# Probabilities turned by a transposing DMA instead of TensorE, with spread stores and earlier last loads

## The chip, the cores and the metric

One core of a Trainium2 chip runs the whole program. The metric is the device time of one execution in microseconds (us); a comparison uses several runs of each kernel on one chip. TensorE does matrix products and transposes (PE in the rows, PEld its weight loads), VectorE is DVE, ScalarE is ACT, GpSimd is POOL, and SyncE (SP) issues nearly all DMA transfers.

## The reference

The reference is a decoder trunk of two layers over 1,024 tokens of width 1,024, in float32. Each layer has a mixer with 16 attention heads and then a mixture of experts; a final RMS norm ends the program. Cut to what the change touches:

```
# 8 heads "fox" (d = 64, decay by a cumulated forget gate), 8 heads "mla" (d = 96, values 64)
s = q_i @ k.T * scale                      # per head and block of 128 queries, causal
s = s + cum[q] - cum[k]                    # fox heads only
p = softmax(where(key <= query, s, -inf))
out_i = p @ v
# mixer: rms_norm of each head, concatenate, @ w_o; h = h + mixer(norm(h)); h = h + moe(norm(h))
# end:   out = rms_norm(h) * final_norm, with h = h + gate_0 * y_0 + gate_1 * y_1 of the last experts
```

## The kernel before

To keep float32 accuracy, an operand is split into a high and a low part and a product is made of three matmuls (`mm3`, L194 to L196). Attention operands are split on the way to DRAM and read back, one head at a time, into a tile `op` (`load_ops`, the DMAs at L93 with the name `op`, some 1.5 MB a head; two buffers, so a head's load waits for the last scores of the head two before it).

A layer's mixer first makes norms and projections (the chunks of `w_in`: v, q, k, each in two halves); `late_pools` then queues the jobs of the mla projections (`qj`, `kj`), and `run(jobs, ...)` puts a few between the matmuls. Their results are stored at L93 as FQ, FK, MQ, MQR, MK.

Attention works in units of up to 1,024 score columns: query block 7 alone, then blocks 6 and 0, 5 and 1, 4 and 2, and block 3 of two heads together. Two heads make a **pair** of 9 units; a layer has 8 pairs, 72 units, four pairs of fox heads and then four of mla heads. One unit goes through these steps:

- `scores` (TensorE, L873 and the causal mask L877) into `S` in PSUM, two buffers;
- `row_max` (VectorE, L885), `expo` (ScalarE, L894: the exponential, into `pr` in SBUF, float32);
- `flip` (8 TensorE transposes L902 into PSUM `pt`; ScalarE L904 takes the high half `ph` in float16, VectorE L905 the low half `pl`);
- `values` (TensorE, L916: three 64-column matmuls for each key block, with `ph` or `pl` as weights).

After the last unit of a head, `fin_a`, `fin_b`, `fin_m` and `fin_c` normalise the output and turn it (L928, L930, L939, L946, L953, L957, L959).

The loop over n (L1001 on) writes `scores(n)`, `row_max(n)`, `flip(n - 1)`, `expo(n)`, `values(n - LAG)` with LAG = 2. The order on TensorE, VectorE, ScalarE and GpSimd is as written. SP's queue is ordered by the library's scheduler and then also runs strictly in order: a DMA that waits holds those behind it.

Each expert weight is loaded, split and multiplied in the mixture of experts, which the change leaves alone. At the end `last_a` (L1653 on) adds two rows `y` of the experts' results per 128 tokens (L225), squares (L1657), and the normed rows are stored (L1665, L1666).

Of the kernel before, what the change touches and what calls it, by code (L numbers as in the profile page):

```python
# [20 lines left out]
P = 128  # L21
# [37 lines left out]
LAG = 2  # L59
PRB = 4  # L60
# [21 lines left out]
def kernel(ctx: ExitStack, tc: tile.TileContext, x, positions, attn_norm, w_in, b_f, q_norm, w_uq,  # L82
# [283 lines left out]
    def mixer(l, opened):  # L366
# [3 lines left out]
        FQ = dram.tile([H, 3 * HD + 4, T], F32R, name=f"FQ{l}")  # L370
        FK = dram.tile([H, 2 * HD + 4, T], F32R, name=f"FK{l}")
# [289 lines left out]
        for dst in (FQ[:, 3 * HD:3 * HD + 2], FK[:, 2 * HD + 2:]):  # L661
            move(dst.rearrange("h r (c t) -> h (r c) t", t=P), one)

        def late_pools():
# [78 lines left out]
            jobs.extend(kj)  # L743
# [6 lines left out]
        for ci, (nm, half) in enumerate(chunks):  # L750
            _, wh, wl = cur
            nxt = prepare(base[chunks[ci + 1][0]] + 256 * chunks[ci + 1][1]) if ci + 1 < len(chunks) else None
            if (nm, half) == ("k", 0):
                late_pools()
# [13 lines left out]
            else:  # L768
                for s in range(4):
# [7 lines left out]
                    def take(nm=nm, j=j, cs=cs, ps=ps):  # L777
                        st = stg.tile([P, 2, 512], F32R, name="st")
                        if nm == "q":
                            split(st[:, 0], st[:, 1], ps, FOX_SCALE)  # L780
                        else:
                            split(st[:, 1], st[:, 0], ps)
                        for e in range(2):
                            h, rs = 2 * j + e, slice(e * HD, (e + 1) * HD)
                            if nm == "q":
                                move(FQ[h, HD:3 * HD].rearrange("(b r) t -> r b t", r=HD)[:, :, cs], st[rs])
                                move(FQ[h, 0:HD, cs], st[rs, 0])
                            else:
                                move(FK[h, 0:2 * HD].rearrange("(b r) t -> r b t", r=HD)[:, :, cs], st[rs])

# [3 lines left out]
                    run(jobs, 4 if nm == "k" else 3)  # L794
# [38 lines left out]
        run(jobs, len(jobs))  # L833
# [54 lines left out]
        def expo(u):  # L888
            u["pr"] = att.tile([P, T], F32, name="pr", bufs=PRB)
            for (h, qb, col), nm in zip(u["segs"], u["nm"]):  # L890
                if h // 2 not in zst:
                    zst[h // 2] = att.tile([P, NT, 2], F32, name="zs", bufs=3)
                s = slice(col, col + (qb + 1) * P)
                act.activation(u["pr"][:, s], u["S"][:, s], AF.Exp, bias=nm, accum_out=zst[h // 2][:, qb, h % 2:h % 2 + 1])  # L894

        def flip(u):
            u["ph"] = att.tile([P, NT, P], F16, name="ph")
            u["pl"] = att.tile([P, NT, P], F16, name="pl")
            for q in range(2):
# [760 lines left out]
    for i in range(NT + 1):  # L1660
        if i < NT:
            last_a(i)
        if i:
            ht, ot, rstd = st[i - 1]
            dve.scalar_tensor_tensor(ot, ht, rstd, gb, op0=OP.mult, op1=OP.mult)  # L1665
            sp.dma_start(out[0, (i - 1) * P:i * P], ot)  # L1666
# [43 lines left out]
```

## Time and profile before

| | us |
|---|---|
| median of 3 runs | 1942.1 (1937.24 to 1949.56) |
| the profiled execution, its own time | 1941.36 |
| its span in the trace | 1939.6 |
| first layer: attention, 72 units | about 245 to 486 |
| second layer: attention, 72 units | about 1189 to 1426 |
| experts, first and second layer | 624 to 940, 1560 to 1880 |
| last stage, after the experts | 1880 to 1939.6 |

The trace has the busy time of each engine in any stretch, the granted clock of TensorE (1.00 is 2.4 GHz, 0.50 is 1.2 GHz), the share of time that the 16 DMA engines were busy, and their rate. A row of a stretch holds its start and end, its length, the busy us (and instructions) of PE, PEld, DVE, ACT and POOL, then the granted clock, the DMA share and GB/s. A pair of fox heads takes 29.0 us (303 to 332), a pair of mla heads 31.3 us (392.3 to 423.6).

### The profile page before, as it was taken

The numbers are of one execution on the slowest core, as the hardware profiler recorded it, in microseconds if no ns is written. First come the engines' busy times: TensorE is split into PE (matmuls) and PEld (weight loads), VectorE is DVE, ScalarE is ACT, GpSimd is POOL, SyncE is SP. The second block draws the span as 40 slices with busy tenths as digits, with TensorE's granted clock in tenths as the row PEclk, the third lists the DMA queues.
The fourth block names the chain that finished last, engine by engine and source line by source line (L and its number), as shares of the span: only waits on it lengthen the run. The fifth ranks groups of instructions, "written<-read, shape, count | busy, mean of one in ns | idle before, by whom it ended". The sixth has DMA issues, their size and how long they took to land.

```text
span 1939.6 us, 33742 instructions
## 1 busy us (share of the span) xinstructions
PE 1742.0 (90%) x12509; PEld 1410.5 (73%) x12509; DVE 1362.6 (70%) x2180; ACT 1184.9 (61%) x2254; POOL 587.2 (30%) x849
## 2 busy tenths in 40 slices
PE   7999899999996999999499997999999979999960
PEld 6987678888785777666399876888878757776640
DVE  6463478888336999888565345888863689998855
ACT  4442378888312898878344334888861268888751
POOL 4001145233313334332331021532241243343315
PEclk9999989999997999999799998999999979999995
DMA  5247833453763999999742776344547479999986
GB/s 162 66 114 213 274 134 111 101 121 88 248 210 135 359 357 353 362 353 357 273 156 53 185 242 219 110 121 107 119 144 251 153 268 365 350 347 358 351 298 221
DMA packets 145380, 427.11 MB, mean 220 GB/s; under 512 B 22166, under 2 KB 37564, under 8 KB 142140
## 3 DMA queue, kind: packets, MB, share of 16 engines
q1 hardware_dynamic: 129788, 387.14, 60.5%
q0 software_dynamic: 14336, 33.58, 5.2%
q10 hardware_dynamic: 1088, 4.19, 0.6%
q8 instruction: 100, 1.64, 0.4%
q14 instruction: 68, 0.56, 0.1%
HBM read 347.24 MB, written 94.37 MB: 228 GB/s over the span
## 4 chain that ended last, share of the span: by engine, by line
PE 60%; DMA 24%; DVE 6%; ACT 6%; issue 2%; POOL 1%; SPq 1%; POOLq 0%; ACTq 0%; DVEq 0%
PE ps L194 9%; PE ps L195 9%; PE ps L196 9%; DMA gu<-in_w_gate_dram 8%; PE S L873 8%; DMA gu<-in_w_up_dram 6%; PE pt L902 6%; DMA dn<-in_w_down_dram 6%; PE y L916 3%; PE gu L195 2%; PE gu L196 2%; PE gu L194 2%; ACT pr L894 2%; PE y L1140 1%; DVE nm L885 1%
## 5 line engine op out<-in xcount | busy, mean ns | idle before, releaser
L1482 DVE TENSOR_TENSOR lo<-gu,hi 128x1024 fp32r<-128x1024 f32 x248 | 298.0, 1221 | 42.1 <-ACT hi L1481 41.3
L1481 ACT ACTIVATE hi<-gu 128x1024 fp32r<-128x1024 f32 x248 | 257.9, 1059 | 29.7 <-DMA gu<-in_w_up_dram 21.1
L873 PE MATMUL S<-op 96*128 96x512 f32 (+3 forms) x960 | 228.8, 372 | 18.2 <-DMA op<-FK 11.6
L885 DVE TENSOR_REDUCE nm<-S 128x1 f32<-128x1024 f32 (+7 forms) x256 | 183.1, 752 | 67.2 <-PE S L877 67.2
L195 PE MATMUL gu<-lo,V 128*96 128x512 f32 x512 | 206.0, 402 | 11.9 <-DVE lo L1482 11.5
L894 ACT ACTIVATE pr<-S,nm 128x1024 f32<-128x1024 f32 (+7 forms) x256 | 189.2, 755 | 36.3 <-DVE nm L885 36.1
L194 PE MATMUL gu<-hi,V 128*96 128x512 f32 x512 | 206.8, 404 | 1.2 <-ACT hi L1481 0.6
L196 PE MATMUL gu<-hi,V 128*96 128x512 f32 x512 | 204.0, 399 | 0.9 <-DVE V L185 0.3
L904 ACT ACTIVATE ph<-pt 128x512 f16<-128x512 f32 x288 | 157.3, 601 | 66.6 <-PE pt L902 65.7
L1531 POOL DMA_INDIRECT y<-V,sidx x64 | 81.9, 1280 | 372.8 <-ACT V L1530 359.2
L905 DVE SCALAR_TENSOR_TENSOR pl<-pt,ph 128x512 f16<-128x512 f32 x288 | 184.7, 682 | 8.9 <-ACT ph L904 7.8
L873 PEld LDWEIGHTS S<-op 96*128 96x128 f32 (+1 forms) x960 | 161.3, 196 | 35.7 <-DMA wor<-in_w_o_dram 6.9
L1482 DVE TENSOR_TENSOR lo<-dn,hi 128x1024 fp32r<-128x1024 f32 x128 | 156.1, 1221 | 18.4 <-ACT hi L1481 14.8
L902 PE MATMUL pt<-ident,pr 128*128 128x128 f32 x1152 | 155.2, 278 | 8.6 <-DVE pl L905 3.5
L1481 ACT ACTIVATE hi<-dn 128x1024 fp32r<-128x1024 f32 x128 | 135.0, 1056 | 21.5 <-DMA dn<-in_w_down_dram 21.3
L902 PEld LDWEIGHTS pt<-ident,pr 128*128 128x128 f32 x1152 | 125.4, 143 | 13.9 <-ACT pr L894 13.0
L195 PEld LDWEIGHTS gu<-lo,V 128*96 128x96 f32 x512 | 83.5, 163 | 58.6 <-DVE lo L1482 29.0
L916 PE MATMUL y<-V,ph 128*128 128x64 f16 x2304 | 121.6, 193 | 2.8 <-ACT ph L904 1.6
L916 PEld LDWEIGHTS <-ph 128*128 128x128 f16 x2304 | 116.9, 98 | 5.3 <-ACT ph L904 1.8
L916 PE MATMUL y<-V,pl 128*128 128x64 f16 x1152 | 117.0, 193 | 1.1 <-DVE pl L905 1.0
L196 PEld LDWEIGHTS gu<-hi,V 128*96 128x96 f32 x512 | 83.4, 163 | 38.3 <-DVE V L185 6.2
L175 POOL TENSOR_SCALAR rs_v<-ss 128x1 f32<-128x1 f32 (+1 forms) x44 | 20.6, 468 | 289.6 <-ACT xn L1096 150.5
(363 smaller groups left out, 4366.0 us busy)
## 6 DMA issues: line engine op xcount, KB each, us to landing
gu<-in_w_gate_dram SPq DMA_DIRECT2D x124, 512.0 KB
gu<-in_w_up_dram SPq DMA_DIRECT2D x124, 512.0 KB
dn<-in_w_down_dram SPq DMA_DIRECT2D x60, 1024.0 KB
raw<-in_w_in_dram SPq DMA_DIRECT2D x48, 256.0 KB
h<-ht SPq DMA_DIRECT2D x17, 512.0 KB
FQ<-st SPq DMA_DIRECT2D x32, 256.0 KB
FK<-st SPq DMA_DIRECT2D x32, 256.0 KB
MQ<-st SPq DMA_DIRECT2D x16, 512.0 KB
```

The source lines that it names most:

```text
L194: pe.matmul(ps, sh(kc), mh(kc), start=first and i == 0, stop=False)
L195: pe.matmul(ps, sh(kc), ml(kc), start=False, stop=False)
L196: pe.matmul(ps, sl(kc), mh(kc), start=False, stop=last and i == n - 1)
L873: pe.matmul(o, a[0:k, qs], b[0:k, c0:c0 + n], start=bank not in started, stop=pi == len(passes) - 1 and not diag, skip_group_check=True)
L885: dve.tensor_reduce(nm, u["S"][:, col:col + (qb + 1) * P], axis=AX.X, op=OP.max, negate=True)
L894: act.activation(u["pr"][:, s], u["S"][:, s], AF.Exp, bias=nm, accum_out=zst[h // 2][:, qb, h % 2:h % 2 + 1])
L902: pe.transpose(pt[:, b], u["pr"][:, (4 * q + b) * P:(4 * q + b + 1) * P], ident)
L904: act.activation(u["ph"][:, ks], pt, AF.Copy, scale=P_SCALE)
L905: dve.scalar_tensor_tensor(u["pl"][:, ks], pt, P_SCALE, u["ph"][:, ks], op0=OP.mult, op1=OP.subtract)
L916: pe.matmul(yst[h][:, qb], a[:, b], v[:, kb, h % H, c], start=first_y[h], stop=(kb == qb and s == 2), skip_group_check=True)
L1481: act.activation(h_, raw, AF.Copy)
L1482: eng.tensor_tensor(l_, raw, h_.bitcast(F32), op=OP.subtract)
```

## The change

- The exponentials `pr` are split in SBUF: ScalarE copies all 1,024 columns to the high half `pq[:, 0]` in float16 right behind the exponential, VectorE makes the low half in one instruction of 1,024 columns. One DMA with transposition, issued by SP, then turns the 128 x 2,048 halves of a unit (512 KB) from SBUF to SBUF into `pT`. The 8 TensorE transposes of a unit and the reads of PSUM `pt` are gone.
- LAG is 3 instead of 2, `pr` has 2 buffers instead of 4, `pq` and `pT` 3 each.
- FQ and FK are stored once per half in 128 partitions, with one DMA for a tile of 512 columns, and their extra rows (decay and ones) go to FQC and FKC. A fox head's operands are read with six DMAs, of 64 or 4 partitions, in place of four of 128 or 68.
- Operand loads are written after the unit that uses a head's buffer last (units 4 and 8 of a pair), for the head two later.
- `late_pools` comes one chunk earlier (at the second half of q); four of the eight `kj` jobs move behind the chunks, between the matmuls of the mla values.
- At the end all 16 loads of `y` are written first (16 buffers), and the norm and store of rows i come two steps after their sum instead of one.

```diff
-LAG = 2
-PRB = 4
+LAG = 3
+PRB = 2
...
+        FQC = dram.tile([H, 4, T], F32R, name=f"FQC{l}")
+        FKC = dram.tile([H, 4, T], F32R, name=f"FKC{l}")
...
-            jobs.extend(kj)
+            jobs.extend(kj[:4])
+            late["kj"] = kj[4:]
...
-            if (nm, half) == ("k", 0):
+            if (nm, half) == ("q", 1):
                 late_pools()
...
+                        move((FQ if nm == "q" else FK)[j * P:(j + 1) * P, :, cs], st)
...
-                move(o[:, 0], FQ[h, 0:2 * HD])
-                move(o[:, 2], FK[h, 0:2 * HD])
-                move(o[0:HD + 4, 1], FQ[h, 2 * HD:])
-                move(o[0:HD + 4, 3], FK[h, HD:])
+                hs = slice(h * HD, (h + 1) * HD)
+                move(o[0:HD, 0:2], FQ[hs])
+                move(o[HD:, 0], FQ[hs, 0])
+                move(o[0:HD, 2:4], FK[hs])
+                move(o[HD:, 2], FK[hs, 1])
+                move(o[HD:HD + 4, 1], FQC[h])
+                move(o[HD:HD + 4, 3], FKC[h])
...
         def expo(u):
...
+            act.activation(u["pq"][:, 0], u["pr"], AF.Copy, scale=P_SCALE)
 
         def flip(u):
-            for q in range(2):
-                pt = tps.tile([P, 4, P], F32, name="pt")
-                for b in range(4):
-                    pe.transpose(pt[:, b], u["pr"][:, (4 * q + b) * P:(4 * q + b + 1) * P], ident)
-                ks = slice(4 * q, 4 * q + 4)
-                act.activation(u["ph"][:, ks], pt, AF.Copy, scale=P_SCALE)
-                dve.scalar_tensor_tensor(u["pl"][:, ks], pt, P_SCALE, u["ph"][:, ks], op0=OP.mult, op1=OP.subtract)
+            dve.scalar_tensor_tensor(u["pq"][:, 1], u["pr"], P_SCALE, u["pq"][:, 0], op0=OP.mult, op1=OP.subtract)
+            u["pT"] = att.tile([P, 2 * NT, P], F16, name="pT")
+            sp.dma_start(u["pT"], u["pq"].rearrange("p s t -> p (s t)"), transpose=True)
...
-                for h, _, _ in U[n]["segs"]:
-                    if h not in opnd:
-                        opnd[h] = load_ops(h)
                 scores(U[n])
                 row_max(U[n])
+                if n % 9 in (4, 8) and n < N - 9:
+                    h = 2 * (n // 9) + 2 + (n % 9 == 8)
+                    opnd[h] = load_ops(h)
...
+    for i in range(NT):
+        for j in range(2):
+            sp.dma_start(ys[i][j], y_d[DEPTH - 1][j * T + i * P:j * T + (i + 1) * P])
...
-    for i in range(NT + 1):
+    for i in range(NT + 2):
         if i < NT:
             last_a(i)
+        if i > 1:
+            last_b(i - 2)
```

Three places in the order of the instructions. First SP's queue in the first layer's attention, between two heads' operand loads (`op` is a head's operand tile, `pq` the two halves of a unit's probabilities, `pT` these turned). Before:

```order
L93 DMA op<-FQ_155 128x1024
L93 DMA op<-FK_156 128x1024
L93 DMA op<-FQ_155 68x1024
L93 DMA op<-FK_156 68x1024
L93 DMA op<-FQ_155 128x1024
```

After the change:

```order
L905 DMA_TRANSPOSE pT<-pq 128x16x128 x4
L93 DMA op<-FQ_155 64x2048
L905 DMA_TRANSPOSE pT<-pq 128x16x128
L93 DMA op<-FQ_155 64x1024
L93 DMA op<-FK_156 64x2048
L93 DMA op<-FK_156 64x1024
L93 DMA op<-FQC_157 4x1024
L93 DMA op<-FKC_158 4x1024
L905 DMA_TRANSPOSE pT<-pq 128x16x128 x3
```

SP's queue held operand loads alone; now 9 transposing DMAs of a pair stand among them, one between the first part of a head's load and its other five, the next behind these.

Second, ScalarE in the first layer's attention at the end of a pair, where `fin_c` turns the outputs (L957). Before:

```order
L894 ACTIVATE pr,zs<-S,nm 128x512 x2
L957 ACTIVATE mix<-y_2510,gains 128x256 x2
L904 ACTIVATE ph<-pt 128x512 x2
L894 ACTIVATE pr,zs<-S,nm 128x1024
L957 ACTIVATE mix<-y_2510,gains 128x256 x2
```

After the change:

```order
L898 ACTIVATE pr,zs<-S,nm 128x1024
L899 ACTIVATE pq<-pr 128x1024
L957 ACTIVATE mix<-y_2484,gains 128x256 x2
L898 ACTIVATE pr,zs<-S,nm 128x896
L898 ACTIVATE pr,zs<-S,nm 128x128
L899 ACTIVATE pq<-pr 128x1024
L957 ACTIVATE mix<-y_2484,gains 128x256 x2
```

The copy of the high half stood ahead of the exponential and waited for TensorE's transposes; now it stands behind the exponential, and ahead of the copies of L957.

Third, SP's queue in the last stage (`y` are the experts' results, `out_dram` the output). Before:

```order
L224 DMA y<-y_139 128x1024 x7
L1666 DMA out_dram<-ot 128x1024
L224 DMA y<-y_139 128x1024
L1666 DMA out_dram<-ot 128x1024
L224 DMA y<-y_139 128x1024 x2
```

After the change:

```order
L1612 COMPARE_AND_BRANCH
L1612 UNCONDITIONAL_BRANCH
L199 DMA gb<-in_final_norm_dram 128x1024
L1651 DMA y<-y_139 128x1024 x16
L1667 DMA out_dram<-ot 128x1024 x8
L1713 UNCONDITIONAL_BRANCH
```

Loads and stores took turns; now no load stands behind a store.

## Rows read from the trace of the kernel before

**Rows 1.** The page: the chain that ended last, by engine.

```profile
PE 60%; DMA 24%; DVE 6%; ACT 6%; issue 2%; POOL 1%; SPq 1%; POOLq 0%; ACTq 0%; DVEq 0%
```

**Rows 2.** Busy time by stretch: first fox pair, a fox pair, an mla pair.

```profile
245.00:274.00 29.00, 27.35 (x295) 23.27 (x296) 21.73 (x38) 19.74 (x46) 9.43 (x12) 0.84 0.34 113
303.00:332.00 29.00, 27.44 (x366) 23.87 (x363) 25.74 (x42) 24.82 (x60) 17.67 (x27) 1.00 0.32 115
392.30:423.60 31.30, 30.56 (x384) 27.06 (x384) 25.52 (x42) 25.95 (x62) 11.28 (x21) 1.00 0.53 116
```

**Rows 3.** Groups in the fox pair, 303 to 332: busy, mean ns | idle before, releaser.

```profile
L905 DVE SCALAR_TENSOR_TENSOR pl<-pt,ph 128x512 f16<-128x512 f32 x19 | 12.2, 684 | 0.5 <-ACT ph L904 0.3
L885 DVE TENSOR_REDUCE nm<-S 128x1 f32<-128x1024 f32 (+7 forms) x16 | 11.4, 752 | 1.5 <-PE S L877 1.5
L904 ACT ACTIVATE ph<-pt 128x512 f16<-128x512 f32 x19 | 10.4, 602 | 2.7 <-PE pt L902 2.6
L902 PE MATMUL pt<-ident,pr 128*128 128x128 f32 x72 | 9.7, 277 | 1.0 <-DVE pl L905 0.6
...
L916 PE MATMUL y<-V,ph 128*128 128x64 f16 x147 | 7.9, 193 | 0.2 <-DVE mix L959 0.2
...
L959 DVE SCALAR_TENSOR_TENSOR mix<-y,gains,mix 128x256 fp32r<-128x256 f32 x4 | 1.8, 480 | 1.4 <-ACT mix L957 1.4
```

**Rows 4.** By stretch: before the first scores of the two layers.

```profile
1174.70:1188.90 14.20, 5.39 (x24) 3.87 (x22) 5.49 (x10) 4.73 (x9) 0.00 (x0) 0.78 0.92 289
230.60:245.30 14.70, 5.28 (x24) 3.84 (x22) 5.49 (x10) 4.73 (x9) 0.00 (x0) 0.84 0.89 283
```

**Rows 5.** By stretch: the last stage.

```profile
1887.00:1891.00 4.00, 0.00 (x0) 0.00 (x0) 1.98 (x2) 0.00 (x0) 0.00 (x0) 0.50 1.03 416
1895.00:1899.00 4.00, 0.00 (x0) 0.00 (x0) 3.26 (x3) 0.32 (x2) 3.58 (x6) 0.50 0.41 155
1899.00:1903.00 4.00, 0.00 (x0) 0.00 (x0) 3.05 (x4) 1.15 (x2) 3.28 (x6) 0.50 0.59 195
```

**Rows 6.** What SP's queue waited for in the last stage: us, times, longest.

```profile
SPq L1666 <- DVE ot L1665: 33.2, 8, 9.5
```

**Rows 7.** The page's groups: 1,024-column copy and difference from SBUF to SBUF.

```profile
L1482 DVE TENSOR_TENSOR lo<-gu,hi 128x1024 fp32r<-128x1024 f32 x248 | 298.0, 1221 | 42.1 <-ACT hi L1481 41.3
L1481 ACT ACTIVATE hi<-gu 128x1024 fp32r<-128x1024 f32 x248 | 257.9, 1059 | 29.7 <-DMA gu<-in_w_up_dram 21.1
```

**Rows 8.** By stretch: operand loads of a fox head (302 to 311), an mla head.

```profile
301.00:302.00 1.00, 0.88 (x8) 0.74 (x8) 1.00 (x2) 0.75 (x4) 1.00 (x1) 1.00 0.00 0
302.00:303.00 1.00, 1.00 (x30) 0.99 (x27) 0.82 (x3) 0.90 (x2) 0.75 (x4) 1.00 0.90 156
304.00:305.00 1.00, 1.00 (x12) 0.96 (x12) 0.74 (x2) 0.74 (x3) 0.93 (x2) 1.00 1.02 414
306.00:311.00 5.00, 5.00 (x62) 4.54 (x61) 4.17 (x8) 4.20 (x10) 1.31 (x3) 1.00 0.25 100
347.00:353.00 6.00, 5.87 (x62) 5.09 (x63) 4.58 (x8) 4.94 (x13) 0.48 (x2) 1.00 0.99 213
```

**Rows 9.** Timeline, start and us: the program's first load (512 KB) and its reader.

```profile
0.72 0.40 SPq L403 DMA_DIRECT2D cq<-in_x_dram  x1
...
4.25 1.06 ACT L412 ACTIVATE xn<-cq 128x1024 f32<-128x1024 f32 x1 [2.25 <-DMA cq<-in_x_dram]
```

**Rows 10.** The chain of waits: start, us, one matmul of the mla values.

```profile
230.15 0.23 PE ps L195
```

**Rows 11.** Timeline of the last stage: first loads, last sums, last norm.

```profile
1883.38 3.83 SPq L224 DMA_DIRECT2D y<-y  x7
...
1921.58 2.61 DVE L225 SCALAR_TENSOR_TENSOR gu<-y,gates,gu 128x1024 f32<-128x1024 f32 x2 [0.22 <-DMA y<-y]
...
1928.20 1.28 DVE L1665 SCALAR_TENSOR_TENSOR ot<-gu,rs_d,gb 128x1024 f32<-128x1024 f32 x1 [1.82 <-POOL rs_d L171]
```

More of the change, by code (lines that the diff above doesn't have):

```diff
@@ L570, in forget_d @@
             cs = slice(c * 512, c * 512 + 512)
-            for dst, sgn in ((FQ[:, 3 * HD + 2:, cs], None), (FK[:, 2 * HD:2 * HD + 2, cs], -1.0)):
+            for dst, sgn in ((FQC[:, 2:, cs], None), (FKC[:, 0:2, cs], -1.0)):
                 st = stg.tile([P, 2, 512], F32R, name="st")[0:H]
@@ L660, in mixer @@
         one = trix[0:H, None, P:].to_broadcast([H, 16, P])
-        for dst in (FQ[:, 3 * HD:3 * HD + 2], FK[:, 2 * HD + 2:]):
+        for dst in (FQC[:, 0:2], FKC[:, 2:]):
             move(dst.rearrange("h r (c t) -> h (r c) t", t=P), one)
@@ L793, in mixer @@
                     take()
-                    run(jobs, 4 if nm == "k" else 3)
+                    run(jobs, 3)
             cur = nxt
@@ L823, in mixer @@
         take()
+        run(jobs, len(jobs))
         uk = late["uk"]
@@ L832, in mixer @@
             v_take(vraw2[:, i], ps, NT + i)
-        run(jobs, len(jobs))
+            if i < len(late["kj"]):
+                late["kj"][i]()
         opnd[1] = load_ops(1)
@@ L914, in values @@
                     b = col // P + kb
-                    for s, (a, c) in enumerate(((u["ph"], 0), (u["ph"], 1), (u["pl"], 0))):
-                        pe.matmul(yst[h][:, qb], a[:, b], v[:, kb, h % H, c], start=first_y[h],
+                    for s, (a, c) in enumerate(((0, 0), (0, 1), (NT, 0))):
+                        pe.matmul(yst[h][:, qb], u["pT"][:, a + b], v[:, kb, h % H, c], start=first_y[h],
                                   stop=(kb == qb and s == 2), skip_group_check=True)
@@ L1021, in mixer @@
                 rt, rt_close = open_pool(f"rt{l}", space=PSUM)
-            if EXF and n < N:
-                expo(U[n])
             if 0 <= n - FL < N:
                 flip(U[n - FL])
-            if not EXF and n < N:
+            if n < N:
                 expo(U[n])
@@ L1649 @@
     gb = cb.tile([P, D], F32, name="gb")
+    ys = [[cb.tile([P, D], F32, name="y", bufs=2 * NT) for _ in range(2)] for _ in range(NT)]
+    for i in range(NT):
+        for j in range(2):
+            sp.dma_start(ys[i][j], y_d[DEPTH - 1][j * T + i * P:j * T + (i + 1) * P])
     bcast_row(gb, final_norm)
@@ L1653, in last_a @@
     def last_a(i):
-        ht = combined(DEPTH, i, got[0][i], lambda j: cb.tile([P, D], F32, name="y", bufs=8))
+        ht = got[0][i]
+        for j in range(2):
+            dve.scalar_tensor_tensor(ht, ys[i][j], gates[:, j, i:i + 1], ht, op0=OP.mult, op1=OP.add)
         ot = cb.tile([P, D], F32, name="ot", bufs=4)
@@ L1658, in last_a, with last_b @@
         st[i] = ht, ot, mean_rsqrt(ss, 1.0 / D, 1, "1")
-    for i in range(NT + 1):
+    def last_b(i):
+        ht, ot, rstd = st[i]
+        dve.scalar_tensor_tensor(ot, ht, rstd, gb, op0=OP.mult, op1=OP.mult)
+        sp.dma_start(out[0, i * P:(i + 1) * P], ot)
+    for i in range(NT + 2):
         if i < NT:
             last_a(i)
[L1663 to L1666, printed above, removed]
+        if i > 1:
+            last_b(i - 2)
     cb_close()
```

14 lines of the change are left out of this document (3 added, 11 removed).

## The prediction

> **What bounds the kernel now.** I read the page's top first [rows 1]: TensorE holds 60% of the chain that ended last, DMA 24%, VectorE and ScalarE 6% each. An average says little here, so I read three stages apart: attention, the stretch ahead of it, and the end.
>
> Attention, by stretches of one pair of heads [rows 2]: a pair of fox heads takes 29.0 us with TensorE busy 27.4, VectorE 25.7 and ScalarE 24.8; a pair of mla heads 31.3 us with TensorE busy 30.6. The mla pairs are bound by TensorE. In the fox pairs VectorE is close behind it, and its idle time ended on TensorE's scores (1.5 us), on ScalarE's `mix` copy (1.4) and on the copy `ph` (0.5) [rows 3].
>
> Ahead of attention TensorE waits for the first head's operands: 5.28 us busy in 14.7 us, 5.39 in 14.2, while the DMA engines are busy 0.89 and 0.92 of the time [rows 4]. At the end the DMA share falls to 0.41 and 0.59 after 1.03 [rows 5]: SP's queue is in order, and its stores waited 33.2 us for VectorE, with loads behind them [rows 6].
>
> **TensorE's transposes removed.** 72 in a pair, 9.7 us of its busy time [rows 3]. TensorE is left with 17.7 us (fox) and 20.9 us (mla): it is no bound any more, and what follows is.
>
> **VectorE.** Its 18 low halves of 512 columns go, at about 0.64 us each (12.2 us for 19) [rows 3]: 11.6. Nine of 1,024 columns come; the nearest row reads both operands from SBUF, as they will, and takes 1.22 us [rows 7]: 11.0. So 25.7 becomes 25.1 us a pair. The waits for scores and `ph` go with TensorE's load; that for `mix` (1.4) stays. ScalarE's copy of the high half takes 1.06 us [rows 7] against 2 x 0.60 [rows 3], so ScalarE keeps its 24 to 26 us; but the copy now stands ahead of the two `mix` copies, which VectorE waits for. That is 0 to 2.1 us a pair; I take the middle, 1.0. VectorE's pace is then 25.1 + 1.4 + 1.0 = 27.5 us a pair.
>
> **The transposing DMA.** No row shows one. What it moves is 512 KB a unit. Bounds: a load into 128 partitions ran at 414 GB/s, one on few engines at 100 GB/s [rows 8], so 1.3 to 5.2 us. I take 1.3, since it has 128 partitions on both sides like the faster row, and keep the rest for the range. The way from issue to reader of a lone 512 KB load was 3.5 us (0.72 to 4.25) [rows 9]; SP's part in it, 0.40, is taken for the new instruction too. When is it wanted? The low half of unit u is done when VectorE turns to unit u+2. The values of u and then the scores of u+4 must be through TensorE when VectorE comes to u+4, two units or 6.2 us later; TensorE needs some 0.9 and 1.1 us for these (the values of a fox pair keep it busy 7.9 us, the scores the 9.8 that are left, for 9 units) [rows 3]. That leaves 4.2 us for a way of 3.5: hidden, with 0.7 us to spare.
>
> **Operand loads in the same queue.** A load into 64 partitions ran at 213 GB/s with the DMA engines full (0.99) [rows 8]. All of a fox head's main loads now have 64 partitions, as the mla ones had: 1.57 MB, 7.4 us a head, 14.8 a pair. They keep the engines from the transposes. If the fox loads, which alternate between lower and upper partitions, overlap, they take down to 3.8 us. I charge 0.9 us a pair for late transposes; the rival below has the full price. A pair is then 28.4 us: 0.6 less for fox, 2.9 less for mla. With four of each in both layers: 8 x 0.6 + 8 x 2.9 = **28 us less**.
>
> **The end of attention.** Behind the last scores the old way was 8 transposes (about 0.9) + 0.60 + 0.68 = 2.2 us; the new one is 1.06 + 1.22 + 3.5 = 5.8. Nothing covers it: 3.6 us a layer, **7 us more**.
>
> **Spread stores.** TensorE's idle time ahead of the first scores is 9.4 + 8.8 us [rows 4]. FQ is stored without its third copy and FK through 128 partitions, and half of the MK stores now follow the first head's load, so this load meets a shorter queue: 7.4 us and 2.2 around it (3.5 less 1.3). Its cover grows: 24 matmuls of the mla values and 12 of the moved `kj` jobs at 0.23 us each [rows 10], 8.3 us. About 1 us of wait stays, so **16 us less**; 8 to 18 in the range. The jobs moved earlier cost nothing: the same matmuls stand in the same TensorE time.
>
> **Last loads first.** 16 loads of 512 KB at 416 GB/s [rows 5] from 1884 end near 1904; VectorE's last sums began at 1921.6 [rows 11]. Then VectorE is the bound: 24 steps of 1.3 us, from 1889 to about 1920, plus the last rows' norm; the four `ot` buffers hold it up a little, since the first store now stands behind all loads. The last norm was at 1928.2; **8 us less**, 3 to 11.
>
> **Sum.** -28 + 7 - 16 - 8 = -45. The profiled execution took 1941.4 us, 0.7 under the median of 1942.1: 1941.4 - 45 = **1896 us**. With pairs at 26.5 us (no new wait at all) and the better ends of the other terms it would be near 1862; with pairs at 30 about 1922.
>
> **Rivals.**
>
> *A. The gain stops at VectorE and ScalarE.* If ScalarE's copy delays both `mix` steps in full and mla pairs get some of the late transposes, pairs stand near 30 to 31 us and attention gains nothing: +7 - 24, with up to 14 us more, so 1922 to 1940. For it: VectorE's 25.1 against 25.7 is no saving by itself, and fox pairs already run near it.
>
> *B. Slower: operand loads hold up the transposes.* Place: units 4 and 8 of each pair. SP issues a load's first part (2.5 us), one transpose (1.3), then the other five DMAs (4.9): 8.7 us of work. The first transpose comes about 2.4 us after the load (VectorE's `row_max` and low half), the next 3.1 us later, with 8.7 - 5.5 = 3.2 us ahead of it; less the 0.7 to spare TensorE stalls 2.5 us, twice a pair. 27.5 + 5.0 = 32.5 us: 8 x 3.5 + 8 x 1.2 = 38 more, + 7 - 24: **1962**, and with transposes somewhat above 1.3 us up to 2000. It decides once the loss eats the other gains: 16 pairs x (p - 30.15) = 17, at p = 31.2, a stall of 1.9 us a load. For it: loads at a DMA share of 0.99 [rows 8]; against: a stall only counts where TensorE, which has 7 to 10 us to spare a pair, can't catch up, and fox loads may overlap.
>
> *C. Slower: the transposing DMA is no copy.* If it moves small pieces, the queue needs 14.8 + 9t a pair, and the change loses above t = 1.8 us. At 213 GB/s, t = 2.5: 37.3 us a pair, 1941 + 114 - 17 = 2038; at the slow bound, 5.2 us: 61.6 a pair, about 2427. For it: nothing in the trace shows that SP or the engines do this in a plain load's time.
>
> The Trainium skill, DMA: Bandwidth & Descriptors, section Latency and other measured facts, gives a transposing DMA an effective 261 GB/s, or 350 to 400 where the access is contiguous; an estimate by the lower figure is 2.0 us a unit, 32.8 us a pair and 1967 us in all. No run here shows it yet. The skill also speaks against this change: VectorE: DVE Perf Modes, section The three transpose paths, has 1309 ns for a 128 x 128 block by DMA and 390 ns on TensorE, and advises TensorE where PSUM will do; the trace has TensorE at 9.7 us for 72 blocks [rows 3], so with blocks one after another (21 us a unit, an estimate) C would be far worse than its bound.
>
> **Chances.** Forecast (1862 to 1922) 0.48; A 0.14; B 0.23; C 0.15. This kernel's measurement tells about 1% from no change, 1923 to 1962 here. Faster by over 1%: the forecast and the lowest part of A, 0.50. Within: the rest of A and a third of B, 0.19. Slower: the rest of B, and C, 0.31. The range goes from 1866, with 4% below it, to 2030, which takes in A, B and the mild part of C; some 12% lie above.
>
> **What would show it.** Right: no TensorE transposes in attention, TensorE's busy time 18 to 21 us of a pair near 28.4, VectorE idle mostly for `mix`, TensorE's waits for `pT` short; TensorE's wait ahead of the first scores near 1 us; in the last stage one stretch of loads at a DMA share near 1, with no dip. B: waits of `values` for `pT` of 2 to 3 us twice a pair, behind `op` loads. C: these waits in every unit, or SP's queue busy for several us with each transposing instruction. Wrong in another way: TensorE with longer gaps could fall to the 1.2 GHz level; the first fox pair had 0.84 after its wait and yet took 29 us [rows 2].

## The result, and the profile after

The changed kernel takes 2194.8 us (median of 4 runs, 2191.8 to 2197.1) against 1940.3: 1.130 times as long, interval 1.127 to 1.132. The range ended at 2030. The profiled execution has a span of 2192.7 us, 253.1 more than before, and attention holds it all: from the first scores of a layer to its last values 252.7 and 251.7 us became 378.8 and 378.4.

Stretches of the changed kernel, with the columns of [rows 2]: the third (fox) and the seventh (mla) of the first layer's eight pairs, each from the first `row_max` of a pair to that of the next (every pair time below is taken so, fox and mla). Before, these two took 28.9 and 31.0 us.

```profile
322.90:370.23 47.33, 27.58 (x288) 22.74 (x288) 25.12 (x33) 25.44 (x50) 17.75 (x24) 0.64 0.96 171
...
510.48:556.29 45.81, 29.45 (x322) 24.73 (x320) 25.72 (x34) 25.96 (x51) 10.66 (x19) 0.78 0.94 184
```

VectorE's and ScalarE's work came out as forecast (25.1 and 25.4 us), but no engine is busy for two thirds of the pair. The DMA engines are, at a share of 0.96, and TensorE's clock fell to 0.64. Groups of the same fox pair, to be read against [rows 3]:

```profile
L903 DVE SCALAR_TENSOR_TENSOR pq<-pr,pq 128x1024 f16<-128x1024 f32 x10 | 12.2, 1216 | 0.0
L898 ACT ACTIVATE pr<-S,nm 128x1024 f32<-128x1024 f32 (+7 forms) x16 | 11.7, 739 | 15.1 <-DVE nm L888 15.1
L888 DVE TENSOR_REDUCE nm<-S 128x1 f32<-128x1024 f32 (+7 forms) x16 | 11.5, 752 | 12.2 <-PE S L880 12.1
L916 PE MATMUL y<-V,pT 128*128 128x64 f16 x216 | 10.8, 220 | 19.5 <-DMA pT<-pq 19.5
...
L959 DVE SCALAR_TENSOR_TENSOR mix<-y,gains,mix 128x256 fp32r<-128x256 f32 x4 | 1.8, 480 | 7.6 <-ACT mix L957 7.6
```

Each engine waits for the next one in a circle: ScalarE 15.1 us for VectorE's `row_max`, VectorE 12.1 for TensorE's scores, TensorE 19.5 for the turned halves `pT`. Only the last is a transfer. The timeline of this pair around a head's load (start, us, queue or engine, the wait in brackets) shows it:

```profile
318.13 0.46 SPq L93 DMA_DIRECT2D op<-FQ  x1
318.76 4.67 SPq L905 DMA_TRANSPOSE pT<-pq  x1
...
321.76 1.22 DVE L903 SCALAR_TENSOR_TENSOR pq<-pr,pq 128x1024 f16<-128x1024 f32 x1
323.48 0.58 SPq L93 DMA_DIRECT2D op<-FQ  x1
324.11 1.24 SPq L93 DMA_DIRECT2D op<-FK  x2
...
326.31 16.38 SPq L905 DMA_TRANSPOSE pT<-pq  x4
326.67 1.46 PE L916 MATMUL y<-V,pT 128*128 128x64 f16 x24 [6.26 <-DMA pT<-pq]
...
334.72 1.46 PE L916 MATMUL y<-V,pT 128*128 128x64 f16 x24 [4.24 <-DMA pT<-pq]
...
345.36 0.87 PE L916 MATMUL y<-V,pT 128*128 128x64 f16 x24 [2.49 <-DMA pT<-pq]
351.50 1.46 PE L916 MATMUL y<-V,pT 128*128 128x64 f16 x24 [3.47 <-DMA pT<-pq]
359.11 1.46 PE L916 MATMUL y<-V,pT 128*128 128x64 f16 x24 [3.06 <-DMA pT<-pq]
```

The transpose issued at 318.76 has a load's first part ahead of it and reaches TensorE at 326.67, 7.9 us later. The next unit's halves are ready at 322.98; SP, which stays 4.67 us with the transpose before it and issues the other five loads, comes to them at 326.31, and TensorE waits again until 334.72, 8.4 us after that issue. The values then take 1.46 us, against 0.86 at the full clock (granted 0.50 from 326.67 to 328.13, 1.00 from 340.77 to 341.60). The last two waits of the pair, 3.47 and 3.06 us, belong to its second load in the same way. The one of 2.49 us has no load ahead: its transpose was issued at 340.95 and took 4.4 us.

The change's other parts. TensorE's waits ahead of the second layer's first scores, then (same view) the last transposes of the first layer, and one stretch and VectorE's norms in the last stage:

```profile
1306.06 1.45 PE L876 MATMUL S<-op 128*128 128x512 f32 x4 [1.05 <-DMA op<-FK]
1311.26 1.22 PE L876 MATMUL S<-op 128*128 128x512 f32 x2 [3.69 <-DVE mx L630]
```

```profile
603.43 1.23 DVE L903 SCALAR_TENSOR_TENSOR pq<-pr,pq 128x1024 f16<-128x1024 f32 x1 [0.61 <-ACT pq L899]
607.25 2.77 SPq L973 DMA_DIRECT2D wor<-in_w_o_dram  x2
...
610.13 3.38 SPq L905 DMA_TRANSPOSE pT<-pq  x1
615.59 1.46 PE L916 MATMUL y<-V,pT 128*128 128x64 f16 x24 [6.85 <-DMA pT<-pq]
```

```profile
2150.00:2160.00 10.00, 0.00 (x0) 0.00 (x0) 8.39 (x7) 2.30 (x4) 9.09 (x12) 0.50 1.03 410
```

```profile
2156.56 1.28 DVE L1666 SCALAR_TENSOR_TENSOR ot<-gu,rs_d,gb 128x1024 f32<-128x1024 f32 x1 [0.91 <-POOL rs_d L171]
2157.76 2.60 DVE L1658 SCALAR_TENSOR_TENSOR gu<-y,gates,gu 128x1024 f32<-128x1024 f32 x2
2161.26 1.31 DVE L1666 SCALAR_TENSOR_TENSOR ot<-gu,rs_d,gb 128x1024 f32<-128x1024 f32 x1 [0.91 <-POOL rs_d L171]
```

The operands are nearly there when they are wanted (1.05 us); what is left is a wait for VectorE's `mx` (3.69 us). The last unit's halves, ready at 604.66, are issued at 610.13, since two loads of w_o stand ahead in the queue; in the second layer the same pair of loads makes it wait from 1672.12 to 1677.59. In the last stage the loads have no dip (410 GB/s), but the norms come every 4.7 us, the pace of GpSimd's chain of small steps (9.09 of 10 us busy); the kernel before had this pace too (norms at 1895.71, 1900.42 and 1905.13).

### The profile page after: what moved, and what is told of

The parts are those of the page before. It is cut to its first block, busy times and chain, and to the rows that moved or that the text cites. A ratio compares the mean times of both kernels' runs of the same rounds, so it can differ in the third digit from the quotient of the medians.

```text
span 2192.7 us, 31425 instructions
## 1 busy us (share of the span) xinstructions
PE 1752.6 (80%) x11357; PEld 1397.3 (64%) x11357; DVE 1367.8 (62%) x2036; ACT 1196.2 (55%) x2110; POOL 635.3 (29%) x849
## 5 line engine op out<-in xcount | busy, mean ns | idle before, releaser
L916 PE MATMUL y<-V,pT 128*128 128x64 f16 x3456 | 171.7, 219 | 270.6 <-DMA pT<-pq 270.5
L916 PEld LDWEIGHTS <-pT 128*128 128x128 f16 x3456 | 155.8, 116 | 283.2 <-DMA pT<-pq 282.7
L876 PE MATMUL S<-op 96*128 96x512 f32 (+3 forms) x960 | 307.3, 467 | 12.3 <-DVE mx L630 8.5
L876 PEld LDWEIGHTS S<-op 96*128 96x128 f32 (+1 forms) x960 | 221.5, 265 | 40.4 <-DVE mx L630 9.1
L899 ACT ACTIVATE pq<-pr 128x1024 f16<-128x1024 f32 x144 | 152.2, 1057 | 56.8 <-DMA pT<-pq 53.2
L903 DVE SCALAR_TENSOR_TENSOR pq<-pr,pq 128x1024 f16<-128x1024 f32 x144 | 180.6, 1254 | 1.5 <-ACT pq L899 1.5
L940 POOL TENSOR_TENSOR z<-z,ss 128x8 f32<-128x8 f32 x32 | 25.0, 782 | 348.2 <-DVE ss L939 347.5
L195 PEld LDWEIGHTS gu<-lo,V 128*96 128x96 f32 x512 | 83.5, 163 | 59.7 <-DVE lo L1480 30.3
L196 PEld LDWEIGHTS gu<-hi,V 128*96 128x96 f32 x512 | 83.4, 163 | 38.9 <-DVE V L185 6.9
L194 PE MATMUL py<-hi,V 128*96 128x512 f32 x256 | 104.0, 406 | 1.5 <-ACT V L184 1.5
L194 PEld LDWEIGHTS gu<-hi,V 128*96 128x96 f32 x512 | 83.3, 163 | 33.4 <-ACT V L184 1.6
```

The source lines that it names most:

```text
L194: pe.matmul(ps, sh(kc), mh(kc), start=first and i == 0, stop=False)
L195: pe.matmul(ps, sh(kc), ml(kc), start=False, stop=False)
L196: pe.matmul(ps, sl(kc), mh(kc), start=False, stop=last and i == n - 1)
L876: pe.matmul(o, a[0:k, qs], b[0:k, c0:c0 + n], start=bank not in started, stop=pi == len(passes) - 1 and not diag, skip_group_check=True)
L899: act.activation(u["pq"][:, 0], u["pr"], AF.Copy, scale=P_SCALE)
L903: dve.scalar_tensor_tensor(u["pq"][:, 1], u["pr"], P_SCALE, u["pq"][:, 0], op0=OP.mult, op1=OP.subtract)
```

## The experiments

Theories: **E**, the DMA engines' own time for a transpose; **Q**, the loads ahead of transposes in SP's queue; **L** or **R**, the way from the low half to the values, which closes a ring of three units; later **S**, their sum. Where operands or turning are left out, other data reach the experts (from the first layer's last values to the second's first scores: 689 us in the changed kernel, 807 in e9), so pairs are compared there and not whole times. A time without a number of runs is that of a single run; the kernel before took 1938 to 1948 us beside them. Edits are to the changed kernel unless said otherwise.

**e1, copies in place of transposes.**

```diff
-sp.dma_start(u["pT"], u["pq"].rearrange("p s t -> p (s t)"), transpose=True)
+sp.dma_start(u["pT"].rearrange("p a b -> p (a b)"), u["pq"].rearrange("p s t -> p (s t)"))
```

> The changed kernel with a plain DMA of the same 512 KB a unit, SBUF to SBUF, in place of the transposing one (the turning is left out). Theory E (engine time): the transposing DMA keeps the 16 DMA engines busy for about 2.45 us (a lone one at 599 to 602 us moved 211 GB/s at a share of 1.1), a copy for about 1.3; 9 x 1.3 + 14.8 = 26.5 us of DMA in a pair fits under 28, so pairs of 29 to 31 us and 1930 to 1970 us in all. Theory Q (queue): what costs is the place of the transposes behind operand loads in SP's queue, which stays; pairs of 40 us or more and over 2110 us. Theory L (the way): a lone one takes 5.5 us from issue to reader, of which the moving is a part; copies would come down to 4 and pairs to some 36 us, 2050 us.

2127.6 us; pairs of 42.3 and 41.6. E alone is out: the DMA share fell to 0.68, the pairs by 5.0 and 4.2 us only.

```profile
317.64:359.91 42.27, 26.01 (x288) 21.83 (x288) 25.91 (x34) 25.36 (x50) 17.67 (x24) 0.75 0.68 192
```

**e2, no operand loads for 12 of 16 heads.**

```diff
-opnd[h] = load_ops(h)
+opnd[h] = load_ops(h) if h in (8, 9) else opnd[h - 2]
```

> The changed kernel without the operand loads of 12 of the 16 heads a layer (these heads use the operands of the head two earlier; their own data is left out), transposes as they are. E: 9 x 2.45 = 22 us of DMA a pair, which fits: pairs of 28 to 31 us, 1920 to 1980 us. Q: the same, since nothing stands ahead of the transposes. L: the way of a transposing DMA is too long for three units of lag even alone: pairs of 35 us or more, over 2030 us.

2081.8 us; pairs of 39.1 and 39.2. So the loads are not all of it either; L alone foresaw this, and fails to explain the 7 to 8 us that the loads cost.

```profile
309.05:348.11 39.06, 26.42 (x288) 22.08 (x288) 25.97 (x34) 25.23 (x50) 17.66 (x24) 0.75 0.75 120
```

**e3, loads issued by ScalarE** (`act.dma_start` in `move` for heads 2 on).

> The changed kernel with the operand loads of heads 2 on issued by ScalarE instead of SyncE, so that no transpose stands behind one in a queue. E: the 16 engines are the same, so little changes: pairs of 42 us or more, over 2130 us. Q: pairs of 29 to 32 us, 1930 to 1990 us (ScalarE spends up to 5 us a pair on issuing).

2366.7 us, worse than either theory: the same fox pair takes 61.9 us, and transposes that share the engines with another queue's load come up to 20 us late. Why one is held that long is not shown. Waits, 300 to 640 us (us, times, longest):

```profile
PEld L922 <- DMA pT<-pq: 162.6, 21, 20.1
```

**e4, all but the transposes.** LAG 2 and four `pr`; `expo`, `flip` and `values` as in the kernel before.

```diff
-LAG = 3
-PRB = 2
+LAG = 2
+PRB = 4
...
```

> The change with the TensorE transposes of the kernel before put back (LAG 2, PSUM reads, four buffers), and all the rest kept: spread stores, six operand DMAs a fox head, last loads first. The prediction's terms for these are -16 and -8 us: 1918 us, 0.988 of before. If six loads of 64 rows in the same queue cost the fox pairs something, 1925 to 1935; if the stall before the first scores only moves, about 1934.

1927.8 us (4 runs, 1926.3 to 1930.4) against 1942.8: ratio 0.9924, interval 0.9902 to 0.9947, 15 us less. This version beats both kernels. TensorE's longer waits ahead of the two layers' first scores:

```profile
239.72 2.08 PE L876 MATMUL S<-op 128*128 128x512 f32 x4 [4.68 <-DVE mx L630]
...
1174.68 1.32 PE L876 MATMUL S<-op 128*128 128x512 f32 x4 [1.42 <-DMA op<-FK]
1179.75 1.86 PE L876 MATMUL S<-op 128*128 128x512 f32 x4 [3.67 <-DVE mx L630]
```

In the profiled runs the span is 12.3 us shorter: 8.7 between the last matmul of the mla values and the last values of a layer's attention (255.5 and 254.5 us became 251.6 and 249.7), 1.1 from the first `y` load to the end (56.2 to 55.1), the rest spread over projections and experts.

**e5, the DMAs by themselves.** A series behind the last store of the kernel before; a small ScalarE instruction reads each target.

```diff
+    turn(0, 0)              # one transposing DMA, 512 KB
+    gate(1, 1)
+    for i in range(6):
+        turn(i, 1)
+    gate(6, 0)
+    for i in range(6):
+        copy(i, 0)          # SBUF to SBUF, 512 KB
+    ...                     # transposes and loads, copies and loads, loads, two queues
```

> The kernel before, with a series of DMAs behind its last store, in phases that each start when the one before has landed: one transposing DMA of 512 KB alone; six; six copies of 512 KB from SBUF to SBUF; six transposes alternating with loads of 512 KB into 64 partitions in the same queue; copies and loads alternating; six loads; transposes on SyncE's queue beside loads on ScalarE's. Theory E (engine time): transposes 2.4 us apart, copies 1.3, loads 2.5, and a pair of a transpose and a load 4.9 us, the sum. Theory R (a ring of three units, in which the way of a DMA counts): the lone transpose takes 4.4 us to its reader, and a pair with a load more than 4.9 us, near 6. In two queues (9.7 to 25 us from the low half to the values where the loads came from ScalarE) the transposes end only with the loads.

A phase waited in fact only for the first DMA of the one before; with one queue that changes nothing in the distances. Readers of the lone transpose (issued at 1934.75; the second of the row follows at 1940.80) and of the series:

```profile
1934.75 8.05 SPq L1680 DMA_TRANSPOSE bT<-bq  x2
```

```profile
1939.31 0.21 ACT L1692 ACTIVATE scr<-bT 128x1 f16<-128x1 f16 x1 [9.04 <-DMA bT<-bq]
...
1952.68 0.20 ACT L1692 ACTIVATE scr<-bT 128x1 f16<-128x1 f16 x1 [2.28 <-DMA bT<-bq]
1955.15 0.20 ACT L1692 ACTIVATE scr<-bT 128x1 f16<-128x1 f16 x1 [2.26 <-DMA bT<-bq]
...
1960.23 0.21 ACT L1692 ACTIVATE scr<-bT 128x1 f16<-128x1 f16 x1 [1.19 <-DMA bT<-bq]
1961.48 0.21 ACT L1692 ACTIVATE scr<-bT 128x1 f16<-128x1 f16 x1 [1.05 <-DMA bT<-bq]
...
1977.61 0.21 ACT L1692 ACTIVATE scr<-bT 128x1 f16<-128x1 f16 x1 [1.45 <-DMA bT<-bq]
1982.33 0.21 ACT L1692 ACTIVATE scr<-bT 128x1 f16<-128x1 f16 x1 [1.48 <-DMA bT<-bq]
...
2023.46 0.20 ACT L1694 ACTIVATE scr<-bo 64x1 f16<-64x1 f32 x1 [2.35 <-DMA bo<-in_x_dram]
2026.02 0.20 ACT L1694 ACTIVATE scr<-bo 64x1 f16<-64x1 f32 x1 [2.35 <-DMA bo<-in_x_dram]
```

The lone transpose takes 4.56 us to its reader; six come 2.42 us apart on average (1945.39 to 1957.48), copies 1.25, loads into 64 partitions 2.5. SP's issue of the lone one took 1.94 us, less than 2.42, and the DMA share in the series is 1.13, so the DMA engines and not SP set this pace. A transpose and a load take 4.7 us together, about their sum, not the 6 of R. With the loads on ScalarE's queue the last six of each ended at 2062.2, 28.7 us after 2033.5, again near the sum of 29.5: a second queue adds nothing, and shares the engines otherwise. E's prices hold.

**e6, LAG 4** (four `pT`; one w_o buffer, its casts behind each load).

```diff
-LAG = 3
+LAG = 4
...
-u["pT"] = att.tile([P, 2 * NT, P], F16, name="pT")
+u["pT"] = att.tile([P, 2 * NT, P], F16, name="pT", bufs=4)
...
```

> The changed kernel with values four units behind the scores (LAG 4, four pT buffers; w_o rows through one buffer in place of two, with the casts behind each load, to make room). R: the period of a pair is nine times the way round the ring, divided by its units; 45.9 x 3 / 4 = 34.4 us, 16 x 11.5 = 184 us less: 2010 us. E: the engines are full (share 0.97 in attention), so over 2140 us.

2147.5 us; pairs of 42.9 and 43.1. E's side this time: by e5's prices the engines need 9 x 2.42 + 2 x 7.5 = 36.8 us a pair (an estimate), and more lag can't go below.

**e7, LAG 4 and no loads** (e2 and e6 together).

> LAG 4 and the operand loads of 12 of 16 heads left out, as in the run without loads at LAG 3 (pairs of 38.5 us, 2082 us). R: 38.5 x 3 / 4 = 28.9 us a pair, near VectorE's and ScalarE's own 27 to 28: 1930 us. If something other than the way holds these pairs (VectorE's and ScalarE's order, the transposing DMA's issue on SyncE), no more than 30 us less: 2050.

2031.1 us; pairs of 32.1 and 34.1, 7.0 and 5.1 below e2. Without the loads the lag does count, though less than R's quarter.

**e8, TensorE kept busy**: the eight transposes a unit put back ahead of the values, unread.

> The changed kernel with the eight TensorE transposes of a unit put back where they were, ahead of the values, their results read by nobody: 9.7 us a pair of work more for TensorE. In the changed kernel TensorE waits, and its granted clock is 0.56 to 0.84 in attention: a unit's values take 1.46 us in place of 0.86, and the scores behind them some 2.1 in place of 1.1. If that low clock is a large part of the ring, the extra work raises the clock and the time falls by up to 16 x 3 x 1.2 = 60 us, to 2135 to 2180; if not, the transposes add up to 1 us a unit: 2195 to 2330 us.

2204.0 us; pairs of 46.2 and 47.0 at a clock of 0.78 and 0.85, where they were 47.3 and 45.8 at 0.64 and 0.78. A higher clock gains nothing clear here, so the low one is not what holds these pairs in the main.

**e9, copies and no loads** (e1 and e2).

> Both of the first two edits at once, LAG 3: a plain copy of 512 KB a unit in place of the transposing DMA, and the operand loads of 12 of 16 heads left out (turning and these heads' data are left out). DMA work falls to some 9 x 1.25 = 11 us a pair, and nothing stands ahead of a copy. Theory S (the slowness is the sum of the DMA's own time and of the loads ahead of it, both felt as a longer way round the ring of three units): the lone way of a copy, low half to values, was 3.0 us against 4.4 to 5.7 of a transpose, so pairs of 29 to 33 us and 1930 to 1990 us. If the ring's other steps hold it (VectorE's and ScalarE's order, TensorE's low clock), little less than without loads alone: 36 to 38 us, 2050 us or more.

Pairs of 35.8 and 37.6 at a DMA share of 0.33 and 0.35. With nothing ahead of a copy something still holds the ring; S is too short. TensorE still waits for `pT` (the fox pair's row, and its waits as us, times, longest):

```profile
302.47:338.30 35.83, 24.27 (x284) 20.20 (x280) 25.31 (x34) 25.23 (x50) 18.39 (x24) 0.80 0.33 133
...
PE y L916 <- DMA pT<-pq: 8.9, 4, 3.2
```

This run is no dearer than the forecast's prices for a transpose, 1.3 us of the engines and a way of 3.5: copies come 1.25 us apart (e5), those that TensorE waits for reach it 3.0 us after the low half at the least and 3.4 in the median, and this pair loads nothing. Yet it takes 35.8 us and not 27.5.

**e10, copies, each head's load in four parts, one a unit.**

```diff
+due.setdefault(slow[0] + i, []).extend(part)     # part i of a load, i units later
...
+for a, b in due.pop(n, []):
+    move(a, b)
```

> The kernel with copies in place of transposing DMAs, all loads kept, but each head's load written in four parts, one a unit (2.4 us of DMA at most ahead of a copy, where it was 7.4). Total bytes and queue are the same. If the burst of a load ahead in the queue is what the copies wait for (gaps of 4.9 and 5.9 us twice a pair in the run with copies): pairs from 42 to 34 to 36 us, 2127 to some 2020 us. If the DMA's total work counts (26 us a pair): no change, over 2095.

2041.6 us; pairs of 37.5 and 36.8, 5 less than e1 with the same bytes. So the burst counts, as Q says, and with it gone the loads cost copies little (e9 has 35.8 and 37.6).

**e11, transposes, LAG 4, loads in four parts** (e6 and e10's parts).

> Transposing DMAs, LAG 4, and the loads in four parts, one a unit. By the phases measured behind the kernel, transposes 2.42 us apart and 1.57 MB of loads 7.5 us, the DMA engines need 9 x 2.42 + 15 = 36.8 us a pair, whatever the order: with LAG 4 alone pairs took 43 us. S: the bursts go, and pairs come near that floor, 37 to 40 us: 2147 - 16 x 4.5 = 2075, 2050 to 2100. If the parts are in the way of the transposes as much as the bursts: 2130 to 2170.

2116.5 us; pairs of 39.2 and 39.3, 2.4 us above the engines' 36.8.

```profile
316.67:355.88 39.21, 24.90 (x293) 20.13 (x291) 25.56 (x33) 25.35 (x49) 18.89 (x23) 0.80 1.12 197
```

**e12, two units of nine in mla pairs** turned by the DMA, in e4; a load is written behind the transpose before it (the edit's two main lines, with its constants written in).

```diff
+U = [{"segs": s, "dma": i >= 36 and i % 9 in (2, 6) and i < 70} for i, s in enumerate(units)]
+if m + LAG + U[m]["dma"] != n:
+    continue
```

> The version with the ends alone (1927.8), and in the mla pairs, where TensorE is the bound (30.6 of 31.2 us), two units of nine (2 and 6) turned by the DMA, with values three units behind; the loads are written behind them, at units 5 and 0. TensorE has 2 x 1.1 us less: 28.4 of work. DMA work 2 x 2.42 + 15 = 20 us a pair fits, and each transpose has two units, 6.3 us, for its way of 4.6 us. S: pairs of 29.2 us, 8 x 2 = 16 less, 1912 us, 0.984 of before. If a transpose comes late once a pair: 1925 to 1940.

1941.8 us (12 runs, ratio 0.9995, interval 0.9982 to 1.0008): no gain over before, 14 us worse than e4. Only the first mla pair was shorter (30.2 us); the next two took 34.4 and 32.2, though TensorE waited for `pT` only three times in them, 0.6 us at the longest. Its longest stop, 1.9 us, was for VectorE's `ysb` (L959), and its clock was 0.77 behind it (402 to 406 us). That is not all of the loss; what else held them is left open.

**e13 to e15, what holds e9**, each one edit on e9: e13 has the unread transposes of e8, e14 LAG 4 as in e6, e15 this:

```diff
-            act.activation(u["pq"][:, 0], u["pr"], AF.Copy, scale=P_SCALE)    # in expo
...
+            if n < N:                                                         # end of the step
+                high(U[n])
```

> As the run with copies and without loads (LAG 3; its pairs that load nothing took 32.2, 35.8, 37.4 and 37.6 us), with the eight TensorE transposes of a unit put back ahead of the values and read by nobody. The times of whole runs don't compare here, since other data reach the experts; the pairs do. Theory K (clock): in these pairs the granted clock is 0.74 to 0.84 and a unit's scores take up to 1.84 us in place of 0.9; kept busy, TensorE stays near 1.0 and pairs fall by 3 us or more, to 29 to 33. If the clock is only a consequence of waiting: no fall, 35 to 38 us.

> Copies, no loads, LAG 4. If the way of the copy (3.0 us from low half to values) is still what closes the ring of three units: 35.8 x 3 / 4 = 27, so VectorE's and ScalarE's own 26 to 28 hold: 28 to 30 us a pair. If another ring holds (scores, row_max, exponential, copy, with the two buffers of S): little changes, 34 to 37.

> Copies, no loads, LAG 3, and ScalarE's copy of the high half written at the end of a step, behind the mix copies, instead of right behind the exponential. The prediction charged up to 2.1 us a pair for the copy standing ahead of mix (TensorE's next values wait for VectorE's mix). If that is a large part of the 7 us above the forecast's 28.4: 32 to 34 us a pair; if not, 35 to 38.

e13: 32.9 and 37.9 us at a clock of 0.95, so keeping TensorE busy is worth 3 us in the third pair and nothing in the seventh; of the other two pairs without loads the second gains nothing (32.2 and 32.1) and the sixth 2.6 us. e14: 31.6 and 31.1. e15: 33.8 and 32.0. A unit more for the way, and the copy's place, are each worth 2 to 6.5 us.

**e16 and e18, all of these together**: no loads, LAG 4 and the copy behind `mix`, with copies (e16) and with transposes (e18).

> Copies, no loads, LAG 4 and the copy of the high half behind mix: each of the last two alone brought pairs without loads from 35.8 to 31.8 and 32.4 us. If nothing but VectorE's and ScalarE's own work is left, pairs reach the forecast's 27.5 to 28.5; if VectorE's waits for mix and for the exponential stay, 30 to 31.5.

> The same with the transposing DMAs in place of copies (LAG 4, no loads of 12 heads, copy behind mix). LAG 4 and no loads alone had 32.8 us in pairs without loads. DMA work is 9 x 2.42 = 22 us a pair and the way 4.6 us against four units' 12: hidden, so the same as with copies, 28 to 31 us. If the transposes still cost something at this lag: 32 us or more.

Pairs of 28.4 and 30.3 in e16, 29.2 and 30.0 in e18, fox and mla:

```profile
292.10:320.45 28.35, 19.68 (x292) 15.98 (x288) 25.74 (x34) 24.80 (x50) 19.45 (x23) 1.00 0.41 168
...
418.45:448.76 30.31, 24.32 (x313) 20.04 (x310) 26.76 (x33) 26.23 (x54) 13.27 (x19) 0.97 0.46 180
```

```profile
296.83:325.98 29.15, 22.95 (x290) 18.74 (x288) 25.72 (x34) 24.73 (x50) 18.89 (x25) 0.88 0.91 163
...
427.79:457.82 30.03, 25.01 (x318) 21.06 (x315) 26.62 (x33) 25.68 (x52) 13.28 (x19) 0.94 0.93 175
```

With the loads gone a transpose costs a pair no more than 0.8 us over a copy at this lag, at a DMA share of 0.9. The fox pair comes to the forecast's 28.4, in part by luck: that figure has 0.9 us for late transposes and 1.0 for the copy ahead of `mix`, which e16 leaves out, so like for like it is 26.5. The mla pair stays at 30, the number of rival A but not by its mechanism, since the copy is out of the way of `mix` here; what holds it is not shown.

**e17, what of this the real computation allows**: e11 with the copy behind `mix`.

> The real computation with transposing DMAs, LAG 4, loads in four parts and the copy of the high half behind mix. Engine time of the DMAs 36.8 us a pair stays the floor: pairs of 37 to 39.5 us (39.9 without the copy's move), 2080 to 2115 us; still slower than the kernel before.

2114.9 us; pairs of 41.3 and 38.4, where e11 has 2116.5, 39.2 and 39.3. The copy's place gains nothing clear where transposes and loads fill the DMA engines (36.8 us a pair by e5's prices).

Third (fox) and seventh (mla) pair of the first layer in us:

| kernel | transfer | loads | LAG | fox | mla |
|---|---|---|---|---|---|
| before | none (TensorE) | yes | 2 | 28.9 | 31.0 |
| the change | transpose | yes | 3 | 47.3 | 45.8 |
| e8 | transpose, TensorE kept busy | yes | 3 | 46.2 | 47.0 |
| e6 | transpose | yes | 4 | 42.9 | 43.1 |
| e11 | transpose | in parts | 4 | 39.2 | 39.3 |
| e17 | transpose, copy behind `mix` | in parts | 4 | 41.3 | 38.4 |
| e2 | transpose | no | 3 | 39.1 | 39.2 |
| e7 | transpose | no | 4 | 32.1 | 34.1 |
| e18 | transpose, copy behind `mix` | no | 4 | 29.2 | 30.0 |
| e1 | copy | yes | 3 | 42.3 | 41.6 |
| e10 | copy | in parts | 3 | 37.5 | 36.8 |
| e9 | copy | no | 3 | 35.8 | 37.6 |
| e13 | copy, TensorE kept busy | no | 3 | 32.9 | 37.9 |
| e15 | copy, copy behind `mix` | no | 3 | 33.8 | 32.0 |
| e14 | copy | no | 4 | 31.6 | 31.1 |
| e16 | copy, copy behind `mix` | no | 4 | 28.4 | 30.3 |

## Why the prediction was wrong

**The step that failed** is "That leaves 4.2 us for a way of 3.5: hidden, with 0.7 us to spare". Both sides were off. The way of a lone transpose is 4.56 us and not 3.5, since the engines need 2.42 us for it and not 1.3 (e5): a load's row was taken because it had 128 partitions. And the 4.2 us shrank as soon as TensorE waited: at the 1.2 GHz level the values take 1.46 us in place of 0.86, and the 512-column scores behind them 1.84 in place of 0.89, so some 1.5 us less are left (an estimate). With LAG 3 the transposes are late even with no load about (e2: TensorE waits 10.7 us a fox pair for `pT`). The slack was the larger error: in e9 the way is 3.0 to 3.4 us, shorter than the forecast's 3.5, and the pair still takes 35.8 us. Besides the clock, the 4.2 us left out that TensorE's values wait for `mix`, behind the copy (e15). The prediction named the fall of the clock as a way to be wrong, but gave it no price.

**The loads.** Rival B had the place right: waits of TensorE for `pT` behind `op` loads, though two behind each load (6.26 and 4.24, 3.47 and 3.06 us) and not one. Its price of 2.5 us a load came from the forecast's 1.3 us a transpose. With 2.42, transposes and loads together need 36.8 us of engine time a pair, more than any other engine is busy, and a transpose behind a part of a load comes 7.9 to 8.4 us after its issue. The pair's "0.9 us for late transposes" was some 18 us (47.3 less 28.4 is 18.9; 45.8 less 28.4 is 17.4).

**Rivals were taken one at a time.** C's formula, 14.8 + 9t, gives 36.6 us a pair at the measured t, and by the prediction's own sum 1941 + 16 x (36.6 - 30.15) - 17 = 2027, just inside the range. C's sign showed too: SP stays a median of 2.7 us with each transposing instruction. B's stalls came on top of C's price, and the circle of engines made each late transpose a loss for all of them: from a layer's first scores to its last are 360 us, 45.0 a pair, so another 8.4 a pair and 134 in all. With 17 us more than forecast at the end of attention and some 12 less gained elsewhere (below) that is 2190, against 2194.8. No case had both, so the range ended at 2030.

**What held.** Taken by itself the sum of VectorE's and ScalarE's work was right: 25.1 and 25.4 us measured, and with loads, way and the copy's place out of the way a fox pair takes 28.4 us (e16), with transposes 29.2 (e18). That is 1.9 us above VectorE's 25.1 + 1.4, the part of the sum that e16 keeps, so the agreement with 28.4 is in part luck. The charge of 1.0 us for the copy ahead of `mix` was too small in a ring (e9 to e15: 2.1 us fox, 5.6 mla; e14 to e16: 3.2 and 0.8). The mla pairs take 30 us even then, against the forecast's 28.4, so that term would have been about 1 us a pair and not 2.9.

**The other terms.** End of attention: 7 us forecast; from the last scores to the last values 6.9 us became 19.1 and 18.6, 24 us more in both layers together, of which 5.5 in each are the loads of w_o ahead of the last transpose. Spread stores: 16 us forecast, 8 to 18 in the range; e4 has 8.7 of its 12 there, since TensorE's waits fell to 4.7 and 5.1 us and not to 1: VectorE's `mx` was late next, which the prediction did not name. Last loads: 8 us forecast, about 1 measured; "Then VectorE is the bound" was the wrong step, for GpSimd's chain sets 4.7 us a row, and [rows 5] had it at 3.58 of 4.0 us already.

**Other prices.** The Trainium skill, DMA: Bandwidth & Descriptors, section Latency and other measured facts, gives 261 GB/s as the lower rate of a transposing DMA; the estimate by it was 1967 us. Measured were 217 GB/s (512 KB in 2.42 us), and either rate by itself (1967 and 2027 us) misses the time, for the same reason as the sum. The Trainium skill, VectorE: DVE Perf Modes, section Rules for kernel authors, advises TensorE for a 128 x 128 transpose where PSUM will do. These runs agree: with the transposes on TensorE the rest of the change takes 1927.8 us (e4), with the DMA's 2194.8. The prediction's 21 us a unit, with blocks one after another, is not what they show: 16 blocks came in 2.42 us.

## What to carry to other kernels

Before a transfer is put into a loop over engines, add up the engine time of all that the DMA engines move in that stage, at the rate of each kind; only then ask for the way of one. What is hidden must be hidden behind slack that survives the first stall: once TensorE was relieved here, no engine covered for another any more, and each latency in the ring was paid. And price rivals together where one makes the other dearer.

## What the runs showed of the hardware

- A transposing DMA of 512 KB of 16-bit data, SBUF to SBUF, takes 2.42 us of the DMA engines (share 1.13), nearly twice a copy (1.25 us), and keeps SP 1.6 to 2.0 us with its issue when alone; in attention it took up to 8.5 us (median 2.7 in the first layer), where a copy took 0.5:

```profile
L905 SPq DMA_TRANSPOSE pT<-pq x72: 1560/2744/8460, 245.4 to 610.1; - x72
```

- Transposes and loads cost the sum of their times, in one queue or in two; in two, a transpose beside another queue's load came to TensorE up to 20 us late (e3), and in e5 ScalarE needed 20.3 us to get six loads issued, 3.6 of it in the issues themselves:

```profile
2033.33 20.29 ACTq L1686 DMA_DIRECT2D bo<-in_x_dram  x6
```

- A share of 0.96 for the DMA engines says little of their rate: 171 GB/s in the changed kernel's pair, 219 in transposes and loads back to back (share 1.14), 373 in copies (1.02).
